# Output projection's weights: scaled and split beside the projection of v, kept in DRAM, loaded by the context steps

## The chip, the cores and the metric

The kernel runs on one core of a Trainium2 chip. Its time is the device time of one execution in microseconds (us), taken as the median of several runs. A profile is one more execution, recorded by the hardware profiler; its times are us from the first recorded instruction. The engines are PE (TensorE; PEld is its weight load), DVE (VectorE), ACT (ScalarE), POOL (GpSimd) and SP (SyncE), which issues nearly all transfers of this kernel, one after the other in a fixed order.

## The reference, cut to what matters

One layer of a trunk over 1024 latent tokens and 256 context tokens, width 1024. A normed and modulated input goes through one projection (`w_in`); its columns feed a short gated convolution (512 columns of output) and a bidirectional RWKV-7 scan (512 columns). Both outputs together go through the output projection `w_out`, and a gated residual follows; then a convolutional MLP. The gate `g1` comes from the modulation (`ada_w`).

```python
sh1, sc1, g1, sh2, sc2, g2 = split(silu(c) @ ada_w + ada_b)
hc = modulate(rms_norm(ctx, norm1_g), csh1, csc1)
_, ctx_states = mixer_block(hc, lp, (zero, zero), False)      # context: states only
hx = modulate(rms_norm(x, norm1_g), sh1, sc1)
out_x = concat([y_conv, y_rwkv]) @ w_out
x = x + g1 * out_x
x = x + g2 * conv_ffn(modulate(rms_norm(x, norm2_g), sh2, sc2))
return rms_norm(x, final_g)
```

Since g1 multiplies the columns of the product, the kernel multiplies it into the columns of `w_out` before the product.

## The kernel before, in words

Products that need full precision are made of three matmuls of rounded operands: a weight is split into a rounded high part (ACT cast) and the remainder (POOL subtraction), and so is the other operand.

Stages, in the order of the program:

1. Norms and the modulation's first half. The normed input lies in `hx` tiles.
2. The projections. `proj` runs one block of 128 columns over all tokens; `load_w` loads and splits its weights one block ahead (one buffer `wraw`, two of the split parts). A string `OR1` gives the order of the pieces: `k0` to `k3` (projection of k), `a` (an eighth of the modulation's second half), `u` and `x` (a third of the unit-norm of k; `x` takes the last third and then closes the pool `kn` that holds k), and `0` to `3` (projection of v). The gate g1 is written to DRAM by the first two `a` pieces.
3. `decays` and `invert`, for five groups of two token tiles each, the context's group first: elementwise chains per group of columns and direction, small matmuls, and the inversion of 32x32 triangles by 60 short DVE instructions in a row (lines 671 and 673). Their tiles lie in the pool `dq`. The rest of the projections (r, the gate, the convolution's three parts) is traced behind the first group and between, and its matmuls fill TensorE.
4. The steps of the scan (`steps`), each with one chunk per direction: products with the state (`ry`, line 761), copies, a second product (`pu`), its copy (`vu`), and the state's update (`S`, line 788). Four context steps come first, then sixteen latent steps. The output projection of the convolution's half (`conv_out`, product line 907, tile `pco`) and later that of the scan's half (`outp`, tile `po`) are cut into pieces that fill the latent steps.
5. The MLP and the final norm.

The weights of the output projection are made in stage 4. `w_raw(k)` loads block k of `w_out` (128 rows, 0.5 MB) into one of two buffers `xo`; `w_make(k)` multiplies by the gate (`gb1`, DVE line 900), casts (ACT line 901) and subtracts (POOL line 902). Blocks 0 and 1 are loaded ahead of the steps; after context step r, blocks 2r and 2r+1 are made, behind the step's last instructions on each engine (`behind`), and the next two are loaded. Blocks 0 to 3 serve the convolution's half and lie in the pool `cp_` on the right, blocks 4 to 7 the scan's half in the pool `ow` on the left.

Memory is two stacks of pools, one from each end of SBUF. On the right, above the tiles of stage 1 and 2 that stay, stand `hcp` (context's input), `ad` (modulation) and above these `kn`, 60,288 bytes per partition by the sizes of its tiles, until `x` closes it. On the left, `dq` takes about 100,000 bytes and reaches into the places of `hcp`, `ad` and `kn`. A tile that is put over older ones waits for their last readers (`reuse_waits="tile"`). The order of the instructions on each engine is set when the program is built: a planner with costs of its own takes the ready instruction that was traced first.

Of the kernel before, what the change touches and what calls it, by code (L numbers as in the profile page):

```python
# [8 lines left out]
F32 = mybir.dt.float32  # L9
F32R = mybir.dt.float32r  # L10
AF = mybir.ActivationFunctionType
ALU = mybir.AluOpType
# [3 lines left out]
D = 1024  # L16
# [20 lines left out]
XB, XT = 2, 3  # L37
# [6 lines left out]
B2 = ((2, 3), (1, 6))  # L44
B3 = (7, 5)
PA, PL1 = (0,), (6,)
OR1 = "k0 k1 a k2 a k3 a u 0 a u a 1 u a a x 2 a 3"
B4 = dict(pm=(5, 7), px=(0, 4), ph=(4, 0))
CL, AR = 2, 3
PJ1 = (1, 2, 3)  # L50
# [37 lines left out]
def hybrid_kernel(  # L88
# [7 lines left out]
    V, A, G, PE, SY = nc.vector, nc.scalar, nc.gpsimd, nc.tensor, nc.sync  # L96
# [12 lines left out]
    dr = ctx_.enter_context(tc.tile_pool(name="dr", bufs=1, space=DRAM))  # L109
# [44 lines left out]
    vd = dr.tile([NT, 128, 512], F32, name="v_dram")  # L154
    sgd = dr.tile([128, T], F32, name="sg_dram")
    yd = dr.tile([8, 128, 512], F32, name="y_dram")
    ycd = dr.tile([4, 128, T], F32, name="yc_dram")
    gd = [dr.tile([1, D], F32, name=f"g_dram{i}") for i in range(2)]
    x2d = dr.tile([8, 128, D], F32, name="x2_dram")
# [46 lines left out]
    with ExitStack() as s2:  # L206
# [106 lines left out]
        while n_ < NT:  # L313
# [4 lines left out]
                               in1=prm[:, P_N1:P_N1 + 8].unsqueeze(2).to_broadcast([128, 8, 2]), op0=ALU.add, op1=ALU.mult)  # L318
        for g, (t0, n, w) in enumerate(segs3):
            for q in range(2):  # L320
                o = [seg_tile(g, q, i, F32R) for i in range(2)]
# [45 lines left out]
    sa = ExitStack()  # L367
# [15 lines left out]
    for d in range(2):  # L383
# [3 lines left out]
        for i, src in enumerate((rw_w_up, rw_a_up)):  # L387
            raw = stg()
# [3 lines left out]
            r = slice(64 * i, 64 * i + 64)  # L392
# [64 lines left out]
    def ada_rest():  # L457
# [33 lines left out]
            yield  # L491
        V.scalar_tensor_tensor(out=gs2, in0=modc[:, 3, :, 0], scalar=1.0, in1=prm[:, P_N2:P_N2 + 8], op0=ALU.add, op1=ALU.mult)

    pa_ = Banks(pa=PA)
    ada_ = ada_rest()
    un = unit_k()
    for o in OR1.split():
        if o == "u":
            next(un)
        elif o == "a":  # L500
            next(ada_, None)
        elif o == "x":
            next(un, None)
            kn_.close()
        elif o[0] == "k":
            k_cols(int(o[1:]))
        else:
            v_cols(int(o))
# [197 lines left out]
    @contextmanager  # L706
    def behind():

        with ExitStack() as q:
            for i in chain.values():  # L710
                q.enter_context(tc.issue_after(i.ins))
            yield
# [162 lines left out]
    sa = ExitStack()  # L875
    cp_ = sa.enter_context(tc.tile_pool(name="co", bufs=1, side="right", reuse_waits="tile"))
# [7 lines left out]
    ow = so.enter_context(tc.tile_pool(name="ow", bufs=1, side="left", reuse_waits="tile"))  # L884


    gb1 = cp_.tile([128, D], F32, name="gb1")
    SY.dma_start(gb1, gd[0].to_broadcast([128, D]))

    wts, raws_ = {}, {}  # L890

    def w_raw(k):
        raws_[k] = cp_.tile([128, D], F32, name="xo", bufs=XB)
        SY.dma_start(raws_[k], w_out[0, 128 * k:128 * k + 128, :])

    def w_make(k):

        raw = raws_[k]
        hl = wts[k] = [(cp_ if k < 4 else ow).tile([128, D], F32R, name=f"w{'hl'[i]}{k}") for i in range(2)]
        V.tensor_tensor(out=raw, in0=raw, in1=gb1, op=ALU.mult)  # L900
        A.copy(hl[0], raw)
        G.tensor_tensor(out=hl[1], in0=raw, in1=hl[0].bitcast(F32), op=ALU.subtract)

    def product(po, hl, w, sl):
        for k in range(4):
# [132 lines left out]

    stages = {"m": mix, "o": outp, "h": to_h2}
    ppc = Banks(ry=B2[0], pu=B2[1])  # L1040
    w_raw(0)
    w_raw(1)
    for r in range(4):
        steps(ring, [(0, r // 2, r % 2), (1, 1 - r // 2, 1 - r % 2)], ppc, 1)

        with behind():
            w_make(2 * r)
            w_make(2 * r + 1)
        if r < 3:
            w_raw(2 * r + 2)  # L1050
            w_raw(2 * r + 3)
        if r == 1:
            pend.append(conv_out())
            next(pend[0])
# [197 lines left out]
```

## Time and profile before

| | us |
|---|---|
| median of 3 runs | 1689.11 (1687.71 to 1690.62) |
| profiled execution | 1681.7 |
| its span, first to last instruction | 1679.9 |
| PE busy | 1534.4 (91%) |
| DVE busy | 1154.1 (69%) |
| ACT busy | 619.9 (37%) |
| POOL busy | 567.3 (34%) |

The profiled execution is 7.4 us under the median of the runs. The shares are means over stages with different limits: the DVE's 69% holds stretches where it is never idle and the MLP, where TensorE is. What a change in one stage is worth has to be read from that stage.

### The profile page before, as it was taken

How to read it: one execution, taken by the hardware profiler on the slowest of the kernel's cores; microseconds unless marked ns; L12 is line 12 of the kernel's file. 1: busy time of each engine (PE TensorE's matmuls, PEld its weight loads, DVE VectorE, ACT ScalarE, POOL GpSimd, SP SyncE). 2: the span in 40 equal slices, each digit the busy share in tenths (PEclk: the TensorE clock that was granted, in tenths of full speed). 3: DMA queues.
4: the chain of work that ended last, by engine and by line, in shares of the span. 5: the costliest groups of instructions: out<-in, count | busy, mean ns of one | idle time of the engine just before them, and what ended most of it. 6: DMA issues, size and time to landing. Idle time of an engine off the chain costs nothing.

```text
span 1679.9 us, 27373 instructions
## 1 busy us (share of the span) xinstructions
PE 1534.4 (91%) x10567; PEld 1240.1 (74%) x10567; DVE 1154.1 (69%) x1783; ACT 619.9 (37%) x1158; POOL 567.3 (34%) x498
## 2 busy tenths in 40 slices
PE   7699999989898876898788899999999999999997
PEld 2588678767776766787666678888888887788886
DVE  5964526899899987445677678777777777346645
ACT  2654325535545235443454322221112112325323
POOL 2454413433233222412545232222222222545643
PEclk9699999989998867999899999999999999999999
DMA  9396556556665685989643112111111111533531
GB/s 322 110 290 203 173 169 189 170 164 212 209 198 167 219 261 177 335 262 278 187 133 116 51 50 62 41 49 51 50 51 51 51 40 48 190 101 124 175 93 59
DMA packets 233171, 246.93 MB, mean 147 GB/s; under 512 B 18496, under 2 KB 171685, under 8 KB 233041
## 3 DMA queue, kind: packets, MB, share of 16 engines
q1 hardware_dynamic: 232624, 245.02, 46.9%
q8 instruction: 84, 1.38, 0.4%
q14 instruction: 47, 0.38, 0.1%
q0 software_dynamic: 416, 0.16, 0.0%
HBM read 178.79 MB, written 66.33 MB: 146 GB/s over the span
## 4 chain that ended last, share of the span: by engine, by line
PE 51%; DVE 13%; ACT 2%; DMA 2%; issue 2%; POOL 1%; SPq 0%; DVEq 0%; ACTq 0%; POOLq 0%
PE pf L1105 26%; PE pf L1185 13%; PE po L907 2%; PE pco L907 2%; DVE acc L1152 2%; PE pj L355 2%; DVE ti L673 2%; PE ry L761 2%; DVE tmp L671 1%; PE ps L785 1%; PE pu L773 1%; DMA car<-ar_dram 1%; PE ry L753 1%; DVE S L788 1%; PE ry L794 1%
## 5 line engine op out<-in xcount | busy, mean ns | idle before, releaser
L1105 PE MATMUL pf<-h,fhi 128*128 128x512 f32 x1408 | 385.6, 391 | 7.6 <-DVE act L1157 4.1
L1105 PEld LDWEIGHTS pf<-h,fhi 128*128 128x128 f32 x1408 | 265.2, 189 | 64.3 <-DVE act L1157 4.5
L355 PE MATMUL pj<-hx,whi 128*128 128x512 f32 (+1 forms) x976 | 299.7, 385 | 3.0 <-DVE hx L329 1.9
L1152 DVE SCALAR_TENSOR_TENSOR acc<-gp,prm,acc 128x1024 f32<-128x1024 f32 x176 | 272.9, 1552 | 6.0
L106 POOL TENSOR_TENSOR flo<-fraw,fhi 128x1024 fp32r<-128x1024 f32 x50 | 123.2, 2465 | 305.9 <-ACT fhi L105 305.9
L1105 PE MATMUL pf<-h,flo 128*128 128x512 f32 x704 | 224.3, 391 | 0.0
L355 PEld LDWEIGHTS pj<-hx,whi 128*128 128x128 f32 x976 | 180.8, 192 | 39.6 <-issue 3.9
L355 PE MATMUL pj<-hx,wlo 128*128 128x512 f32 (+1 forms) x488 | 187.0, 383 | 0.0
L1185 PE MATMUL pf<-dhi,ahl 128*128 128x512 f32 x640 | 163.1, 389 | 0.3 <-DVE ahl L1177 0.3
L1177 DVE TENSOR_TENSOR ahl<-act,ahl 128x512 fp32r<-128x512 f32 x44 | 86.2, 1970 | 100.1 <-ACT ahl L1176 100.1
L1105 PEld LDWEIGHTS pf<-h,flo 128*128 128x128 f32 x704 | 132.7, 189 | 27.8 <-POOL flo L106 0.2
L105 ACT CAST fhi<-fraw 128x1024 fp32r<-128x1024 f32 x50 | 52.7, 1054 | 267.7 <-issue 162.5
L1185 PEld LDWEIGHTS pf<-dhi,ahl 128*128 128x128 f32 x640 | 120.0, 188 | 25.6 <-DVE ahl L1177 0.8
L106 POOL TENSOR_TENSOR dlo<-fraw,dhi 128x1024 fp32r<-128x1024 f32 x40 | 98.5, 2466 | 92.2 <-ACT dhi L105 91.4
L106 POOL TENSOR_TENSOR wlo<-wraw,whi 128x1024 fp32r<-128x1024 f32 x26 | 64.4, 2477 | 132.9 <-ACT whi L105 131.9
L1150 DVE TENSOR_SCALAR acc<-gp,prm 128x1024 f32<-128x1024 f32 x22 | 42.5, 1932 | 97.2 <-ACT gp L1142 97.2
L355 PEld LDWEIGHTS pj<-hx,wlo 128*128 128x128 f32 x488 | 93.6, 192 | 16.9 <-issue 0.8
L1185 PE MATMUL pf<-dlo,ahl 128*128 128x512 f32 x320 | 89.1, 389 | 0.0
L651 POOL TENSOR_TENSOR car<-car,pcs 128x512 f32<-128x512 f32 (+1 forms) x38 | 39.6, 1055 | 140.8 <-DMA car<-ar_dram 114.7
L105 ACT CAST dhi<-fraw 128x1024 fp32r<-128x1024 f32 x40 | 41.9, 1050 | 105.0 <-PE pf L1185 87.5
L602 PE MATMUL px<-arO,kbO 64*128 64x128 f32 (+1 forms) x640 | 65.5, 308 | 13.2 <-DVE xrO L606 8.9
L602 PEld LDWEIGHTS px<-arO,kbO 64*128 64x128 f32 x640 | 52.5, 205 | 31.4 <-issue 23.2
(292 smaller groups left out, 2620.1 us busy)
## 6 DMA issues: line engine op xcount, KB each, us to landing
araw<-in_ada_w_dram SPq DMA_DIRECT2D x48, 512.0 KB, 5.7
fraw<-in_ffn_w_up_dram SPq DMA_DIRECT2D x46, 512.0 KB, 3.9
fraw<-in_ffn_w_down_dram SPq DMA_DIRECT2D x44, 512.0 KB, 3.6
wraw<-in_w_in_dram SPq DMA_DIRECT2D x26, 512.0 KB, 4.6
lu<-lu_dram SPq DMA_DIRECT2D x20, 512.0 KB, 4.2
kb_dram<-kbT SPq DMA_DIRECT2D x40, 256.0 KB, 4.3
xa_dram<-xa SPq DMA_DIRECT2D x20, 512.0 KB, 4.4
cxa<-xa_dram SPq DMA_DIRECT2D x40, 256.0 KB, 4.2
```

The source lines that it names most:

```text
L105: A.copy(hi, src)
L106: G.tensor_tensor(out=lo, in0=src, in1=hi.bitcast(F32), op=ALU.subtract)
L355: PE.matmul(p[:, :n], w[:, k, :], hsl(i, k, t0, n), start=(k == 0 and first), stop=(k == 7 and last))
L602: PE.matmul(px[:, ch, i, 0:w], kbO[r, i, 2 * ch:2 * ch + 2, :].rearrange("p s n -> p (s n)"), rhs, start=True, stop=True)
L651: F3.tensor_tensor(out=self.ar, in0=self.ar, in1=self.pc.to_broadcast(list(self.ar.shape)), op=ALU.mult)
L673: V.tensor_tensor(out=ti[:, j + 1:32, 0:j], in0=ti[:, j + 1:32, 0:j], in1=tv, op=ALU.add)
L907: m = PE.matmul(po, hl[:, a_, k, :], w[k][b_][:, sl], start=(k == 0 and f), stop=(k == 3 and l))
L1105: PE.matmul(pts[hf], w[:, k, :], h2[hf][i_][:, k, :], start=(k == 0 and f), stop=(k == 7 and l))
L1150: V.tensor_scalar(out=acc, in0=src, scalar1=wcol, scalar2=prm[:, P_FB + f:P_FB + f + 1], op0=ALU.mult, op1=ALU.add)
L1152: V.scalar_tensor_tensor(out=acc, in0=src, scalar=wcol, in1=acc, op0=ALU.mult, op1=ALU.add)
L1177: V.tensor_tensor(out=hl[:, 1, :], in0=asl, in1=hl[:, 0, :].bitcast(F32), op=ALU.subtract)
L1185: PE.matmul(pd[i], hl[:, a_, 128 * q:128 * q + 128], w[w_][:, 512 * nh:512 * nh + 512], start=(f == 0 and s_), stop=(f == NF - 1 and l_))
```

## The change

A new function, `out_weights`, stands in the order of the projections behind the last third of the unit-norm (`x`) and the third block of v, ahead of the last `a` and the last block of v. It opens a pool `wm` in the stack place that `kn` has left: the gate's row spread over 128 partitions (`gb1`, 4 KB per partition), two buffers for a raw block (4 KB each) and two for a split block (8 KB each), 28,672 bytes in all. For each of the eight blocks it loads the raw rows, multiplies on DVE, casts on ACT, subtracts on POOL and stores both parts to a new DRAM tensor `wo_dram` (1 MB per block). The pool is closed with `ad`, ahead of `decays`. The context steps only load the split blocks, one transfer of 1 MB each, straight into their final tiles; the DVE, ACT and POOL work after each step, the two raw buffers and the `behind` orders are gone.

```diff
-OR1 = "k0 k1 a k2 a k3 a u 0 a u a 1 u a a x 2 a 3"
+OR1 = "k0 k1 a k2 a k3 a u 0 a u a 1 u a a x 2 w a 3"
...
+    wod = dr.tile([8, 128, 2, D], F32, name="wo_dram")
...
+    def out_weights():
+
+        wm = sa.enter_context(tc.tile_pool(name="wm", bufs=1, side="right", reuse_waits="tile"))
+        gb1 = wm.tile([128, D], F32, name="gb1")
+        SY.dma_start(gb1, gd[0].to_broadcast([128, D]))
+        for k in range(8):
+            raw = wm.tile([128, D], F32, name="wor", bufs=2)
+            SY.dma_start(raw, w_out[0, 128 * k:128 * k + 128, :])
+            hl = wm.tile([128, 2, D], F32R, name="wol", bufs=2)
+            V.tensor_tensor(out=raw, in0=raw, in1=gb1, op=ALU.mult)
+            A.copy(hl[:, 0], raw)
+            G.tensor_tensor(out=hl[:, 1], in0=raw, in1=hl[:, 0].bitcast(F32), op=ALU.subtract)
+            SY.dma_start(wod[k], hl.bitcast(F32))
...
-    gb1 = cp_.tile([128, D], F32, name="gb1")
-    SY.dma_start(gb1, gd[0].to_broadcast([128, D]))
-
-    wts, raws_ = {}, {}
-
-    def w_raw(k):
-        raws_[k] = cp_.tile([128, D], F32, name="xo", bufs=XB)
-        SY.dma_start(raws_[k], w_out[0, 128 * k:128 * k + 128, :])
-
-    def w_make(k):
-
-        raw = raws_[k]
-        hl = wts[k] = [(cp_ if k < 4 else ow).tile([128, D], F32R, name=f"w{'hl'[i]}{k}") for i in range(2)]
-        V.tensor_tensor(out=raw, in0=raw, in1=gb1, op=ALU.mult)
-        A.copy(hl[0], raw)
-        G.tensor_tensor(out=hl[1], in0=raw, in1=hl[0].bitcast(F32), op=ALU.subtract)
+    wts = {}
+
+    def w_load(k):
+        hl = (cp_ if k < 4 else ow).tile([128, 2, D], F32R, name=f"w{k}")
+        SY.dma_start(hl.bitcast(F32), wod[k])
+        wts[k] = [hl[:, i] for i in range(2)]
...
-    w_raw(0)
-    w_raw(1)
+    w_load(0)
+    w_load(1)
     for r in range(4):
         steps(ring, [(0, r // 2, r % 2), (1, 1 - r // 2, 1 - r % 2)], ppc, 1)
-
-        with behind():
-            w_make(2 * r)
-            w_make(2 * r + 1)
         if r < 3:
-            w_raw(2 * r + 2)
-            w_raw(2 * r + 3)
+            w_load(2 * r + 2)
+            w_load(2 * r + 3)
```

## Rows read from the trace of the kernel before

**Rows 1.** Stretches: length, busy per engine (instructions), granted clock, DMA share, GB/s

```profile
236.00:248.00 12.00, 12.00 (x56) 10.01 (x55) 0.23 (x1) 3.33 (x4) 2.39 (x1) 1.00 0.85 288
248.00:305.00 57.00, 57.00 (x355) 46.03 (x354) 35.51 (x72) 33.48 (x67) 18.31 (x34) 1.00 0.60 176
305.00:590.00 285.00, 253.11 (x2175) 203.98 (x2175) 270.98 (x625) 130.52 (x246) 94.69 (x146) 0.92 0.64 193
590.00:602.00 12.00, 10.67 (x178) 9.32 (x174) 6.00 (x13) 4.34 (x6) 1.24 (x2) 0.51 0.98 277
602.00:652.00 50.00, 28.06 (x476) 25.09 (x478) 47.68 (x84) 17.97 (x35) 14.71 (x10) 0.63 0.65 205
667.00:695.00 28.00, 21.86 (x318) 17.87 (x316) 12.60 (x19) 12.41 (x24) 11.83 (x7) 0.94 1.02 348
```

**Rows 2.** Groups of DVE instructions in 602 to 652: busy, mean ns, idle before

```profile
L900 DVE TENSOR_TENSOR xo<-xo,gb 128x1024 f32<-128x1024 f32 x4 | 4.7, 1222 | 0.1
```

**Rows 3.** Timeline of DVE, inversion: start, length, line, tile, shape

```profile
607.68 0.32 DVE L673 TENSOR_TENSOR ti<-ti,tmp 128x150 f32<-128x150 f32 x1
...
619.62 2.44 DVE L671 TENSOR_TENSOR tmp<-ti 128x240 f32<-128x240 f32 x1
...
622.81 1.72 DVE L673 TENSOR_TENSOR ti<-ti,tmp 128x240 f32<-128x240 f32 x1
...
626.49 0.41 DVE L673 TENSOR_TENSOR ti<-ti,tmp 128x238 f32<-128x238 f32 x1
...
639.10 2.36 DVE L673 TENSOR_TENSOR ti<-ti,tmp 128x150 f32<-128x150 f32 x1
...
642.54 2.31 DVE L673 TENSOR_TENSOR ti<-ti,tmp 128x130 f32<-128x130 f32 x1
```

**Rows 4.** Timeline of POOL: the first two subtractions; two more start at 638.85 and 642.32

```profile
619.28 4.98 POOL L902 TENSOR_TENSOR wl<-xo,wh 128x1024 fp32r<-128x1024 f32 x2 [10.14 <-ACT wh L901]
```

**Rows 5.** Timeline, latent steps: PE's state product; DVE's multiplication with the wait ahead

```profile
677.55 2.02 PE L761 MATMUL ry<-S,car 128*128 128x128 f32 x16 [2.07 <-DVE S L788]
...
688.97 2.55 DVE L900 TENSOR_TENSOR xo<-xo,gb 128x1024 f32<-128x1024 f32 x1 [1.31 <-DMA xo<-in_w_out_dram]
...
694.94 2.05 PE L761 MATMUL ry<-S,car 128*128 128x128 f32 x16
706.39 2.05 PE L761 MATMUL ry<-S,car 128*128 128x128 f32 x16
```

**Rows 6.** Timeline of POOL and of SP's queue where `dq` follows `kn`

```profile
235.63 0.15 POOL L570 MEMSET P<- 128x4 f32 x2 [6.78 <-PE pb L440]
...
236.26 0.33 SPq L442 DMA_DIRECT2D kk_dram<-kkr  x1
236.65 0.59 SPq L531 DMA_DIRECT2D dxl<-xl_dram  x1
```

**Rows 7.** SP's queue where the tiles of `conv_out` follow `dq`

```profile
666.47 1.01 SPq L701 DMA_DIRECT2D xa_dram<-xa  x2
...
668.21 3.58 SPq L918 DMA_DIRECT2D x<-in_x_dram  x3
```

**Rows 8.** Timeline: multiplications of blocks 0 and 1, the load into the freed buffer

```profile
616.90 2.36 DVE L900 TENSOR_TENSOR xo<-xo,gb 128x1024 f32<-128x1024 f32 x2
...
621.81 2.82 SPq L894 DMA_DIRECT2D xo<-in_w_out_dram  x2
```

**Rows 9.** Tile xo: issue to landing of its transfers, all of them

```profile
DMA to landing us min/median/max: 3.8/6.2/8.4
```

**Rows 10.** Groups of DVE instructions of the convolution's columns, whole span

```profile
L841 DVE TENSOR_TENSOR cu<-pj,cu 128x512 f32<-128x512 f32 x8 | 5.5, 686 | 1.3 <-PE pj L355 1.2
L843 DVE TENSOR_SCALAR cy<-cu,prm 128x1024 f32<-128x1024 f32 x4 | 3.9, 972 | 0.0
L845 DVE SCALAR_TENSOR_TENSOR cy<-cu,prm,cy 128x1024 f32<-128x1024 f32 x8 | 10.2, 1275 | 0.0
L849 DVE TENSOR_TENSOR cy<-pj,cy 128x512 f32<-128x512 f32 x8 | 5.4, 681 | 0.1
```

More of the change, by code (lines that the diff above doesn't have):

```diff
@@ L504, in hybrid_kernel @@
             kn_.close()
+        elif o == "w":
+            out_weights()
         elif o[0] == "k":
```

## The prediction, made before the changed kernel was run

> **What bounds the kernel now.** I read the page for the two stages that the change touches, then cut the span into stretches with one limit each, and only then looked at single instructions. The page's means say little here: the DVE's 69% is made of stretches at 98% and stretches at 45%. In the stretches [rows 1] the reader should compare PE's and DVE's busy time with the length. From 236 to 305 TensorE is full (12.00 of 12, 57.00 of 57) and DVE has room (0.23 of 12, then 35.5 of 57): projections are the limit and the context's decays run at their pace. From 305 to 590 DVE works 271 of 285 us, TensorE 253. So DVE is the limit there, and it stays it until 652 (47.7 of 50), while the last inversion and the context steps share it. Between them lie 12 us with DVE half idle and DMA at 0.98. From 667 to 695 DMA stands at 1.02 (348 GB/s), and no engine is full.
>
> **What is removed.** Of the eight blocks, four are made inside the DVE's full stretch. Their multiplications take 4 x 1.22 = 4.9 us, with 0.1 us of idle time ahead of them [rows 2]: that is path. POOL's four subtractions cost DVE more than that. During them an instruction of the inversion that takes 0.32 to 0.41 us takes 2.44, 1.72, 2.36 and 2.31 [rows 3, 4]. The four are 2.0 + 1.3 + 2.0 + 2.0 = 7.4 us longer than their like. Together -12.3 us; the bounds are -4.9 (if the stretching has another cause) and -12.3. The ACT casts lie beside and count nothing. Blocks 6 and 7 are made in the latent steps: DVE's multiplication waits for its transfer, and the copies of the step are queued behind it. The step from 677.55 to 694.94 takes 17.4 us, the next one 11.4 [rows 5]; without the multiplications I let the first fall to the second, -5.9 us, with bounds 0 and -5.9, since DMA is full there [rows 1] and may hold the step anyway.
>
> **What is moved, and where it lands.** The pass issues 8 multiplications (9.8 us), 8 casts, 8 subtractions and 17 transfers on SP's queue. As work it would cost nothing: DVE is free in 236 to 248 and TensorE is the limit [rows 1]. (Without that cover it would cost the 9.8 us and the stretching of whatever DVE does beside the subtractions.) What counts is the memory it stands in. `wm` takes the stack place of `kn`, and `dq`, with all tiles of the decays, comes over the same place later. The trace shows both halves of this. POOL's first memset of a decay tile (P) waits 6.8 us for a matmul of the unit-norm, which reads a tile of `kn` (bc8); by the sizes of the tiles, bc8 ends 17,280 bytes from the end of `kn` that stays, so P lies inside the 28,672 bytes of `wm` too. And the first load of the decays is issued 0.39 us behind the last store of `kn` [rows 6], though what it loads was written long before; the loads of `conv_out` follow the last store of `dq` in the same way [rows 7]. I read this as: the planner gives out a pool's place only when the last instruction of the pool beneath has been issued. Then `wm` begins at about 237, and the decays begin when the last store to `wo_dram` has been issued.
>
> How long is the pass? A raw buffer turns over in a load and 4.9 us (multiplication at 616.90, next load into the buffer at 621.81 [rows 8]). The load took 3.8 to 8.4 us, median 6.2 [rows 9]. Four rounds on each of two buffers: 4 x (6.2 + 4.9) = 44.4 us; 35 and 53 at the ends. I take the median, since the pass fills DMA as its old place did. So the decays start at 282 in place of 237: **+45 us** (36 to 54). As traffic the pass is 25 pieces of 0.524 MB, 13.1 MB, which at the 348 GB/s of [rows 1] is 38 us, inside those ends. The Trainium skill, page "SBUF — State Buffer", section "Summary: rules for kernel authors", says to reckon transfers between HBM and SBUF at about 358 GB/s; by that alone the pass would be 37 us (an estimate) and the forecast 8 us lower. The trace's best stretch, 348 GB/s, agrees with that figure, but the pass is a chain of loads and instructions, so I keep the chain.
>
> Part of this comes back. TensorE does not stop in the pause: 56 matmuls in 12.00 us [rows 1] make a column of 48 some 10.3 us, so 45 us put the projections 4.4 columns ahead. DVE's work on the convolution's 12 columns is 5.5 + 3.9 + 10.2 + 5.4 = 25.0 us [rows 10], 2.1 per column; 4.4 of them leave the full stretch: -9 us (0 to -9). DVE's idle time from 305 to 652 is 14.0 + 6.0 + 2.3 = 22 us [rows 1]; with 45 us less of TensorE's work beside it some of this closes: -5 us (0 to -22; I stay near zero, as most waits there are for copies and transfers that remain). The rest of the pause stays, because DVE is full from 305 on and has no other room to catch up.
>
> **What is added later.** SP loses nine transfers and gets eight, each twice as large. `cp_` opens when the last projection is done, and nothing holds blocks 1 to 3 back any more, where the two raw buffers did: 4.19 MB in place of 1.57 in a stretch with DMA at 0.98. The 2.6 MB more are 9.5 us at its 277 GB/s [rows 1]; I count +2 (0 to 9.5), as the chain needs only some of what is queued behind. Blocks 4 to 7 lie in `ow`, over `dq`, so by the reading of [rows 7] they come all together at the end of the inversion, just where DMA is full: 3.1 MB more, 9 us at 348 GB/s. In SP's queue the chunks of the next steps and the rows of x stand behind them, and DVE's residual add, with the state's update behind it, waits for x. I count +3 (0 to 9).
>
> **The sum.** 45 - 9 - 5 - 12.3 - 5.9 + 5 = +17.8 us on the profiled execution, 1681.7, gives 1699.5. That execution is 7.4 us under the median of the runs; put back on, 1707.
>
> **The rivals.**
> 1. *The pass hides, and the kernel is faster.* For it: the work is covered (DVE idle, TensorE full), and tiles of `kn` come free one by one, so that the planner could start the pass earlier and let the decays take places that the pass has left or never used. It decides at one point: whether the decays' first load is issued ahead of the last store to `wo_dram`, by so much that DVE has its usual work from 248 on. Then -12.3 - 5.9 + 5 and some 2 us for DVE's stretched instructions: -11, so 1678. Against it: [rows 6, 7]. The Trainium skill's page "SBUF — State Buffer", section "Who interferes with whom", speaks for this rival: "DMA never contends with a compute engine", so 16 MB more traffic would slow no instruction. The trace does not contradict it: where DMA is at 0.98, engines wait for data, they do not run slower. Chance 0.18.
> 2. *The pause is absorbed.* If DVE's full stretch has more give than I think (all 22 us of idle time close), the sum is 45 - 9 - 22 - 12.3 - 5.9 + 5 = +1, so 1690. For it: TensorE is at 89% in that stretch and will be relieved. Against it: DVE's own 95% there. Chance 0.12.
> 3. *It costs more.* The full 54 us of the slowest loads, with stores in SP's queue that wait for POOL while weight loads stand behind them, and nothing of the idle time back: 54 - 9 - 12.3 - 5.9 + 10 = +37, so 1726. Chance 0.10.
>
> **How the numbers follow.** My forecast, a pause carried mostly to the end, has 0.60, at 1707, by itself from about 1695 to 1721 (no idle time back: +32). A measurement of this kernel can tell some 0.2% (3.4 us) from no change. Slower by more: 0.60 + 0.10 = 0.70; within it 0.12; faster 0.18. For 8 in 10 the range goes from 1684, which leaves most of the first rival out, to 1724, which leaves out half of the third.
>
> **What would show it.** Right: on SP's queue the first load of `xl_dram` directly behind the last store to `wo_dram`, near 280; DVE nearly idle until about 290 but for eight multiplications; DVE full from some 350 on. In the steps no instruction of the inversion above 1.5 us, and the inversion's end 10 to 25 us later than 652. The second latent step shorter than 17.4 us. Wrong: decays that start before 260 (rival 1), an inversion that ends within a few us of its old time though the decays started late (rival 2), or a first latent step that waits for x longer than before, which would put the price into DMA.

## The result, and the profile after

| | before | after |
|---|---|---|
| median of the runs, us | 1689.86 (1687.71 to 1693.30) | 1729.94 (1728.35 to 1733.60) |
| profiled execution, us | 1681.7 | 1730.15 |
| its span, us | 1679.9 | 1728.2 |

The ratio is 1.025, with a 95% interval of 1.023 to 1.027 (the two medians by themselves give 1.024): the changed kernel is 40 us slower. The prediction had the side (slower, 0.70) and missed the size: 1707, with a range that ended at 1724. The profiled execution of before lies 8.2 us under the median of these four runs, and under every other run of this kernel on record (1683.1 to 1695.2); that of after lies at its median. So differences between the two traces are some 8 us larger than those of the medians (48 against 40).

First the stretches of after, as in [rows 1]: start and end, length, busy time of PE, PEld, DVE, ACT, POOL (instructions), granted clock, DMA share, GB/s.

```profile
251.00:295.00 44.00, 44.00 (x196) 36.46 (x195) 8.18 (x6) 15.77 (x19) 27.06 (x14) 1.00 0.97 345
295.00:350.00 55.00, 55.00 (x313) 45.09 (x313) 33.89 (x63) 26.16 (x53) 18.39 (x27) 1.00 0.59 179
350.00:500.00 150.00, 135.34 (x1063) 108.27 (x1063) 140.27 (x315) 63.24 (x121) 53.55 (x77) 0.97 0.56 172
500.00:550.00 50.00, 36.61 (x452) 30.74 (x445) 46.57 (x119) 24.18 (x49) 13.74 (x27) 0.69 0.88 293
550.00:600.00 50.00, 29.79 (x412) 26.09 (x412) 34.49 (x81) 21.42 (x39) 13.63 (x26) 0.61 0.94 288
600.00:650.00 50.00, 39.83 (x268) 33.34 (x268) 49.09 (x136) 21.92 (x46) 14.86 (x24) 0.60 0.60 172
655.00:692.00 37.00, 24.33 (x483) 21.73 (x477) 33.99 (x78) 13.13 (x29) 4.54 (x4) 0.73 0.59 190
708.00:750.00 42.00, 31.72 (x402) 26.04 (x399) 10.77 (x21) 12.29 (x28) 3.83 (x4) 0.87 1.04 358
```

The first line is the pass: TensorE full, DMA full, DVE at 8 of 44. The second looks like the 57 us from 248 in [rows 1], 47 us later. The fifth line is the surprise: DVE, forecast to be full from 350 on, is idle for 15.5 of 50 us, with DMA at 0.94. The last line is the place of the first latent steps: 358 GB/s, no engine full.

SP's queue of after around the pass (start, length, line, transfer), which answers [rows 6]:

```profile
239.32 0.33 SPq L443 DMA_DIRECT2D kk_dram<-kkr  x1
239.70 0.44 SPq L499 DMA_DIRECT2D gb<-g_dram  x1
240.24 0.87 SPq L502 DMA_DIRECT2D wor<-in_w_out_dram  x2
...
251.82 0.33 SPq L507 DMA_DIRECT2D wo_dram<-wol  x1
...
291.89 0.32 SPq L507 DMA_DIRECT2D wo_dram<-wol  x1
294.24 0.38 SPq L339 DMA_DIRECT2D wraw<-in_w_in_dram  x1
294.68 0.73 SPq L548 DMA_DIRECT2D dxl<-xl_dram  x1
```

Before, 0.4 us lay between the last store of `kk_dram` and the decays' first load [rows 6]. Now it is 294.68 - 239.32 = 55.4 us, and in between stands the whole pass. The load is issued 58.0 us later than before; 3.1 of these lie ahead of the pass.

The line of the pass's multiplications, with the idle time of DVE ahead of them (us, times):

```profile
L504 DVE TENSOR_TENSOR wor<-wor,gb x8: 1212/1240/2564, 245.7 to 287.1; 128x1024 f32<-128x1024 f32 x8
its engine sat idle before it (us, times) until:
  DMA wor<-in_w_out_dram: 28.4, 6
  POOL wlo L106: 8.7, 1
```

The multiplications wait mostly for their own loads: 28.4 us of idle time ahead of them, in six waits.

The end of the last inversion (its last stream transposition, DVE), in before and in after:

```profile
649.26 1.94 DVE L679 STREAM_TRANSPOSE rti<-ti 128x1024 f32<-128x1024 f32 x1
```

```profile
690.53 1.92 DVE L696 STREAM_TRANSPOSE rti<-ti 128x1024 f32<-128x1024 f32 x1
```

So a delay of 58 us at the decays' start is 41 us here, and 48 us at the end of the span. TensorE's products with the state that begin the second to the fifth latent step of after; the second to the fourth of before are in [rows 5], and the fifth stands last here:

```profile
711.17 2.05 PE L778 MATMUL ry<-S,car 128*128 128x128 f32 x16
721.51 3.65 PE L778 MATMUL ry<-S,car 128*128 128x128 f32 x16
749.61 3.37 PE L778 MATMUL ry<-S,car 128*128 128x128 f32 x16
762.33 2.05 PE L778 MATMUL ry<-S,car 128*128 128x128 f32 x16
```

```profile
717.78 2.05 PE L761 MATMUL ry<-S,car 128*128 128x128 f32 x16
```

The second product is 33.6 us late, less than the inversion's end; the fifth is 44.6 us late. So some 3 of the 7 us are lost up to here and the other 4 behind it. The step that was forecast to become shorter did: 10.3 us in place of 17.4 [rows 5]. The next one takes 28.1 us in place of 11.4, and the three steps together 51.2 in place of 40.2.

DVE's residual add in that long step, with the wait ahead of it, and the longest such wait in before:

```profile
726.50 1.29 DVE L942 TENSOR_TENSOR x<-pco,x 128x512 f32<-128x512 f32 x2 [7.57 <-DMA x<-in_x_dram]
```

```profile
675.94 0.69 DVE L935 TENSOR_TENSOR x<-pco,x 128x512 f32<-128x512 f32 x1 [3.54 <-DMA x<-in_x_dram]
```

### The profile page after: what moved, and what is told of

It is laid out like the page before. It is cut to its first block, busy times and chain, and to the rows that moved or that the text cites. A ratio compares the mean times of both kernels' runs of the same rounds, so it can differ in the third digit from the quotient of the medians.

```text
span 1728.2 us, 27381 instructions
## 1 busy us (share of the span) xinstructions
PE 1559.1 (90%) x10567; PEld 1264.7 (73%) x10567; DVE 1139.8 (66%) x1783; ACT 618.3 (36%) x1155; POOL 572.5 (33%) x498
## 4 chain that ended last, share of the span: by engine, by line
PE 48%; DVE 10%; DMA 3%; ACT 1%; issue 1%; POOL 1%; DVEq 0%; SPq 0%; ACTq 0%; POOLq 0%
PE pf L1108 26%; PE pf L1188 12%; PE po L914 2%; PE pco L914 2%; PE ry L778 2%; DVE acc L1155 2%; DMA x<-in_x_dram 1%; PE ry L770 1%; DVE ti L690 1%; DVE tmp L688 1%; PE pu L790 1%; DVE S L805 1%; DMA cxr<-xr_dram 1%; PE ps L802 1%; PE ry L811 0%
## 5 line engine op out<-in xcount | busy, mean ns | idle before, releaser
L356 PE MATMUL pj<-hx,whi 128*128 128x512 f32 (+1 forms) x976 | 294.8, 382 | 5.4 <-DVE hx L330 3.0
L1108 PEld LDWEIGHTS pf<-h,flo 128*128 128x128 f32 x704 | 133.3, 189 | 28.1 <-POOL flo L106 0.5
L356 PEld LDWEIGHTS pj<-hx,wlo 128*128 128x128 f32 x488 | 92.9, 190 | 16.7 <-issue 0.6
L619 PE MATMUL px<-arO,kbO 64*128 64x128 f32 (+1 forms) x640 | 72.9, 343 | 16.7 <-DVE xrO L623 13.1
L619 PEld LDWEIGHTS px<-arO,kbO 64*128 64x128 f32 x640 | 59.8, 237 | 32.1 <-issue 23.3
```

The lines of the kernel that those rows point to most:

```text
L356: PE.matmul(p[:, :n], w[:, k, :], hsl(i, k, t0, n), start=(k == 0 and first), stop=(k == 7 and last))
L619: PE.matmul(px[:, ch, i, 0:w], kbO[r, i, 2 * ch:2 * ch + 2, :].rearrange("p s n -> p (s n)"), rhs, start=True, stop=True)
L1108: PE.matmul(pts[hf], w[:, k, :], h2[hf][i_][:, k, :], start=(k == 0 and f), stop=(k == 7 and l))
```

## The experiments

Two theories stood against each other. A: the pass is the price, since the decays wait for the memory in which it stands. B: the loads of 1 MB blocks are the price, since they fill DMA ahead of what the steps need. In the runs "pass alone", "no pass" and "early pass" the letters mean these two; every other expectation defines an A and a B of its own. Each kernel ran beside the kernel before on the same chip; ratios go against that.

| kernel | median, us | ratio to before | 95% interval |
|---|---|---|---|
| changed kernel | 1729.94 | 1.0251 | 1.0229 to 1.0273 |
| pass alone | 1728.99 | 1.0258 | 1.0238 to 1.0277 |
| no pass | 1690.63 | 1.0022 | 1.0008 to 1.0035 |
| early pass | 1702.68 | 1.0105 | 1.0069 to 1.0142 |
| blocks 4 to 7 traced later | 1732.61 | 1.0279 | 1.0255 to 1.0302 |
| no pass, blocks 0 to 3 held | 1686.67 | 0.9990 | 0.9973 to 1.0007 |
| no pass, all blocks held | 1682.50 | 0.9969 | 0.9951 to 0.9987 |
| early pass, all blocks held | 1684.10 | 0.9973 | 0.9955 to 0.9991 |
| changed, ring held | 1729.44 | 1.0228 | 1.0192 to 1.0265 |
| changed, ring and blocks held | 1715.21 | 1.0164 | 1.0119 to 1.0209 |
| pass on ACT's queue | 1719.30 | 1.0199 | 1.0179 to 1.0220 |
| half the store | 1719.64 | 1.0204 | 1.0185 to 1.0222 |

**The pass alone.** The kernel before, with the pass in it and its result unused:

```diff
-OR1 = "k0 k1 a k2 a k3 a u 0 a u a 1 u a a x 2 a 3"
+OR1 = "k0 k1 a k2 a k3 a u 0 a u a 1 u a a x 2 w a 3"
+        elif o == "w":
+            out_weights()
```

> The kernel before with the pass added as the change has it, and its result used by nobody: the context steps still load, multiply and split the blocks themselves. So it has the change's cost without its gain. Theory A (the decays wait for the memory of the pass, and that delay is carried to the end): in the trace of the changed kernel the first load of xl_dram is issued at 294.7 in place of 236.7, and nothing of it came back by the end of the inversion but what was removed from the context steps. Then 1689 + 45 to 55 = 1735 to 1745, slower than the changed kernel (1730) by some us. Theory B (the delay is mostly absorbed by the stretches behind it, and the loads of 1 MB blocks are the price): not above 1705. First load of xl_dram near 292 to 295 in both.

The ratio, 1.0258, is that of the changed kernel: the pass alone costs as much as the whole change. Theory B's limit, 1705, is far off. Theory A holds for the pass, though the median, 1729, is under its 1735 and not above the changed kernel's: some of the delay does come back, and the removed work is worth nothing net, as the next run shows. The first load of `xl_dram` on SP's queue and the end of the last inversion on DVE, in this trace:

```profile
290.34 0.73 SPq L548 DMA_DIRECT2D dxl<-xl_dram  x1
```

```profile
700.00 1.91 DVE L696 STREAM_TRANSPOSE rti<-ti 128x1024 f32<-128x1024 f32 x1
```

53.7 us late at the decays' start, 50.7 at the inversion's end, 47.0 at the end of the span. All that DVE's full stretch gave back is 3 us.

**No pass.** The changed kernel without it, the blocks loaded from another tensor of the same size:

```diff
-OR1 = "k0 k1 a k2 a k3 a u 0 a u a 1 u a a x 2 w a 3"
+OR1 = "k0 k1 a k2 a k3 a u 0 a u a 1 u a a x 2 a 3"
-        SY.dma_start(hl.bitcast(F32), wod[k])
+        SY.dma_start(hl.bitcast(F32), xld[:, :, 0:D])
```

> The changed kernel without the pass: the context steps load 1 MB per block from xl_dram in place of wo_dram, so the output projection's weights hold other numbers and the multiplication, the split and the store are left out altogether. Same loads, same tiles, same order of the steps. Theory A (the pause is the price, the removed work a gain): the inversion's end comes 10 to 14 us earlier than in the kernel before (651), the step in which blocks 4 to 7 are loaded stays some 28 us long, and the time is 1675 to 1690. Theory B (the loads are the price): 1705 or more, with DVE idle for 10 us and more in the last 50 us ahead of the last inversion.

Neither: 1691, between the two. The inversion's end does not come earlier (649.33), and the longest of the first latent steps takes 21.1 us. The work of eight multiplications, casts and subtractions is gone, nothing was put in its place but loads, and the kernel is no faster. DVE's timeline of this kernel shows why:

```profile
612.23 0.75 DVE L623 TENSOR_TENSOR xrO<-px,cst 128x256 f32<-128x256 f32 x2 [4.67 <-DMA xr_dram<-xrO]
612.90 1.90 DVE L682 STREAM_TRANSPOSE ti<-xb 128x1024 f32<-128x1024 f32 x1
...
649.33 1.94 DVE L696 STREAM_TRANSPOSE rti<-ti 128x1024 f32<-128x1024 f32 x1
```

The same transposition at the start of the last inversion, in before:

```profile
602.04 1.97 DVE L665 STREAM_TRANSPOSE ti<-xb 128x1024 f32<-128x1024 f32 x1 [0.41 <-ACT xb L661]
```

The last inversion begins 10.9 us later than before. From the end of the fourth inversion to there DVE waits 6.8 us for stores of the last group's decays to land, so that their buffers are free (3.7 us in before), and 7.4 us for products of TensorE (1.8 in before); DMA stands at 1.05 in 602 to 613. Then inversion and context steps take 36.4 us in place of 47.2. The gain of some 11 us is there, and it is taken away just ahead of it; whether the loads do that is what the next run asks. The stretching by POOL's subtractions is gone too: 30 instructions of a line of the inversion, minimum, median and maximum in ns, first in before (590 to 700), then here.

```profile
L671 DVE TENSOR_TENSOR tmp<-ti x30: 168/372/2440, 604.1 to 647.0; 128x30 f32<-128x30 f32 x2, 128x58 f32<-128x58 f32 x2, 128x84 f32<-128x84 f32 x2, 128x108 f32<-128x108 f32 x2
```

```profile
L688 DVE TENSOR_TENSOR tmp<-ti x30: 167/358/730, 614.9 to 647.1; 128x30 f32<-128x30 f32 x2, 128x58 f32<-128x58 f32 x2, 128x84 f32<-128x84 f32 x2, 128x108 f32<-128x108 f32 x2
```

The Trainium skill, page "SBUF — State Buffer", section "Who interferes with whom", says that a DVE instruction with two inputs in SBUF contends with a GpSimd instruction that reads SBUF. The maximum, 2440 ns with subtractions beside it and 730 without, agrees.

**Blocks 0 to 3 held.** The kernel without the pass, with these loads behind a copy that waits for a context step:

```diff
-    def w_load(k):
+    def w_load(k, behind_):
         hl = (cp_ if k < 4 else ow).tile([128, 2, D], F32R, name=f"w{k}")
+        if behind_ is not None:
+            G.tensor_copy(hl[:, 0, 0:8], behind_)
...
+        if r < 2:
+            w_load(2 * r, Sd[0][:, 0, 0:8])
+            w_load(2 * r + 1, Sd[0][:, 0, 0:8])
```

> The kernel without the pass (blocks loaded from xl_dram, multiplication, split and store left out, as before), and one thing more: the loads of blocks 0 to 3 are held behind the first two context steps (a copy of 8 columns of the state into the block's tile, ahead of its load), so that they no longer stand in DMA while the last group's decays run. Theory A (in the kernel without the pass these 4 MB make DVE wait for a store of xr_dram from 606.0 to 612.2, and the last inversion begins at 613.0 in place of 602.0, which takes back all that the removed work gives): the inversion begins at 600 to 605 and ends (last rti copy) at 637 to 642 in place of 649, and the time is 7 to 12 us under that of the kernel without the pass (1691), some 1679 to 1684, below the kernel before. Theory B (the last stretch has another limit, and the removed work lay beside it): the inversion's end stays at 647 to 652 and the time at 1687 to 1694.

Theory A holds for the place: the inversion begins and ends where it was expected to, and the loads account for 7.8 of the 10.9 us.

```profile
605.13 1.94 DVE L682 STREAM_TRANSPOSE ti<-xb 128x1024 f32<-128x1024 f32 x1
...
640.81 1.95 DVE L696 STREAM_TRANSPOSE rti<-ti 128x1024 f32<-128x1024 f32 x1
```

The end comes 8.5 us earlier than without the hold. Only 4 of these reach the end of the kernel (1686.7, not the 1679 to 1684 expected): the step between the state products at 667.16 and 692.93 takes 25.8 us, with blocks 4 to 7 and the rows of x in the same stretch.

**All blocks held.** Blocks 4 to 7, too, each behind a residual add:

```diff
+            if 1 <= n <= 4:
+                w_load(3 + n, xts_[t][:, 0:8])
```

> As the kernel before this one, and blocks 4 to 7 are held as well: each behind the residual add of one of the second to fifth tiles of the convolution's half, so some 30 to 80 us later, and one at a time. Still without the pass and with other numbers for the weights. Theory A (the 4 MB stand ahead of the x rows): the latent step of 19.3 us falls to 11 to 15 and the time is 4 to 8 us under that of the kernel with blocks 0 to 3 held alone. Theory B (the x rows and the chunks fill DMA there by themselves): no more than 2 us.

The end of the last inversion:

```profile
639.18 1.97 DVE L696 STREAM_TRANSPOSE rti<-ti 128x1024 f32<-128x1024 f32 x1
```

The state products now stand at 663.93, 679.33 and 691.44: 25.8 us became 15.4, and the median fell by 4.2 us, the lower end of theory A. Later steps take most of the lead back: against the kernel with blocks 0 to 3 held the products are 13.6 us ahead at 679.33 and 3.7 us at 758.66, with a step of 17.4 us between. So without any pass, and with the loads out of the way, the removed work is worth 0.3%, 5 us. That is all that the change could win with these holds.

**Blocks 4 to 7 traced later.** In the changed kernel the loads were moved behind the latent steps 4 to 7 in the program:

```diff
-        if r < 3:
+        if r < 1:
             w_load(2 * r + 2)
             w_load(2 * r + 3)
...
+        if 4 <= r < 8:
+            w_load(r + 0)
```

> The changed kernel with one thing moved: blocks 4 to 7 are loaded one by one behind the latent steps 4 to 7, no longer together at the end of the inversion; they are first used behind step 10. Theory A (these 4 MB stand in SP's queue and in DMA ahead of the x rows for which DVE's residual add, and the state's update behind it, waits): the step of 28.1 us (721.5 to 749.6) falls to 14 to 18, and the time is 1715 to 1722. Theory B (DMA is full there anyway with the chunks of the steps and the x rows): the step stays above 24 us and the time within 4 us of 1730.

Inconclusive as it was meant: the planner takes what is ready, and the loads were issued at 726.94 to 733, only 14 us later, still in the full stretch. The long step did shrink (715.43, 734.53, 753.40, 766.53), but three steps together take 51.1 us, as in the changed kernel (711.17 to 762.33: 51.2). I read this as: in a full stretch it is the bytes that count, not which of them comes first. Hence the copies that wait, above. One thing this run does show, the wait for x:

```profile
725.86 1.29 DVE L942 TENSOR_TENSOR x<-pco,x 128x512 f32<-128x512 f32 x2 [7.64 <-DMA x<-in_x_dram]
```

It ends before the first of the four blocks is issued and is as long as in the changed kernel. So the wait does not need these blocks ahead of it.

**Early pass.** The same pass in 12 KB on the left, in 16 pieces of 512 columns, in the projections of k and v:

```diff
+    we = sa.enter_context(tc.tile_pool(name="we", bufs=1, side="left", reuse_waits="tile"))
-OR1 = "k0 k1 a k2 a k3 a u 0 a u a 1 u a a x 2 w a 3"
+OR1 = "k0 a k1 a k2 w k3 w a w u w 0 w a u w a w 1 w u a a x 2 a 3"
```

> The changed kernel with the same pass elsewhere: 12 KB per partition on the left, free during the projections of k and v, in 16 pieces of 512 columns, from behind k2 on, so that nearly all of it is through when the unit-norm ends. Nothing else differs. Theory A (place in memory and time of the pass): the first load of xl_dram is issued 0 to 15 us later than in the kernel before, and the time is 1680 to 1700, as for the kernel without the pass plus that delay. Theory B (16 MB more traffic and the pieces on SP's queue are what costs, wherever they stand): the projections of k and v take 10 us and more longer, and the time stays above 1710.

The median, 1703, is a little above theory A's range and far under theory B's. Most of the price is gone with the place; the same 13 MB of traffic elsewhere cost far less. (The trace is of the slowest of the four runs, 1712.) The waits of DVE from 80 to 256 (us, times, longest) have this line:

```profile
DVE wor L505 <- DMA wor<-in_w_out_dram: 29.4, 9, 4.8
```

The pass's multiplications wait for their loads with the unit-norm queued behind them on DVE. The last store of `kk_dram` comes at 248.31 in place of 236.26, and the first load of `xl_dram` at 255.66, 19 us late, a little more than expected; here too it follows the last store of the pass (252.87). That the waits are what delays the unit-norm is not shown: in the last run below they fall to 11.9 us, and the last store of `kk_dram` comes no earlier (250.11).

**Pass on ACT's queue.** Is it the memory that the decays wait for, or the place in SP's queue?

```diff
-            SY.dma_start(wod[k], hl.bitcast(F32))
+            A.dma_start(wod[k], hl.bitcast(F32))
```

(and so for the two loads in the function)

> The changed kernel with the pass's 17 transfers issued from ACT's queue in place of SP's. Theory A (the decays wait for the memory that the pass stands in, when its last instruction has been issued): the first load of xl_dram is still issued behind the last store to wo_dram, at 288 to 298, and the time is 1722 to 1740. Theory B (they wait in SP's queue, in which the pass's stores stand ahead of their loads and wait for POOL): the load comes at 236 to 250, and the time falls to 1685 to 1700.

ACT's queue, then SP's, of this kernel:

```profile
290.07 0.33 ACTq L507 DMA_DIRECT2D wo_dram<-wol  x1
```

```profile
292.42 0.38 SPq L339 DMA_DIRECT2D wraw<-in_w_in_dram  x1
292.85 1.03 SPq L548 DMA_DIRECT2D dxl<-xl_dram  x1
```

SP has nothing of the pass in its queue, and its load still follows the last store, 55.3 us behind the last store of `kk_dram` (237.60). So it is not the order in SP's queue, and the place in memory, as [rows 6, 7] were read, is what is left. The Trainium skill, page "DMA: Bandwidth & Descriptors", section "Issuing engines are not separate DMA queues", says that transfers run on the same 16 engines whoever issues them; 55.3 us here and 55.4 from SP's queue agree. The median, 1719, is 10 us under the changed kernel's and in neither range; the gain appears between the decays' third and fourth group, and I did not find its cause.

**Half the store.** What makes the pass 55 us long?

```diff
-            SY.dma_start(wod[k], hl.bitcast(F32))
+            SY.dma_start(wod[k, :, 0], hl[:, 0].bitcast(F32))
-        SY.dma_start(hl.bitcast(F32), wod[k])
+        for i in range(2):
+            SY.dma_start(hl[:, i].bitcast(F32), wod[k, :, 0])
```

> The changed kernel with half the store: the pass stores the rounded half of a block only, 0.5 MB in place of 1 MB, and the context steps load that half into both places, in two transfers of 0.5 MB; the remainder is made, but left out of the product. It asks what sets the length of the pass (239.7 to 294.7). Theory A (DMA: 345 GB/s in 251 to 295, of which the projections' weights and the stores of r are a part, so 4.2 MB less are 12 us): the first load of xl_dram at 280 to 285, the time 8 to 12 us under the changed kernel's 1730. Theory B (the chain of a buffer: load, multiplication, cast, subtraction, next load): the load comes at 290 to 295, the time within 4 us of 1730.

SP's queue at the end of the pass:

```profile
281.53 0.55 SPq L507 DMA_DIRECT2D wo_dram<-wol  x1
283.44 0.32 SPq L845 DMA_DIRECT2D sg_dram<-stg  x1
283.81 0.58 SPq L548 DMA_DIRECT2D dxl<-xl_dram  x1
```

283.81 less 236.61, the last store of `kk_dram`, is 47.2 us, 8.2 less than with the full store, and the median falls by 10. DMA's share in 252 to 280 falls from 1.02 to 0.75. Not all of the 8.2 us is traffic: the store of the rounded half no longer waits for POOL's subtraction, which takes some 3.5 us off the end (the last subtraction ends at 285.03, the last store is issued at 281.53). So the traffic of the full store is worth some 5 us of the pass. With the full store 18.3 MB move between 238 and 295; 13.1 MB of them are the pass's, the other 5.2 MB the projections' own weights and stores.

**Ring held.** Why did DVE's full stretch give so little back? In the changed kernel the third inversion's last transposition stands at 559.4 against 519.8, 40 us late in place of 58, and the fourth's at 649.1 against 588.4, 61 us late: 18 us had come back, and then were lost again.

```diff
+    def hold():
+        z = wp.tile([128, 8], F32, name="zh")
+        for g in (1, 2):
+            for q in range(2):
+                for i in range(2):
+                    G.tensor_tensor(out=z, in0=hxt[g, q, i][:, 0, 0:8].bitcast(F32), in1=groups[6][:, 0, 0, 0, 0:8], op=ALU.add)
...
+            if ti == 6 and n == 0:
+                hold()
```

> The changed kernel with one thing more: eight small POOL additions read the projections' input tiles and wait for the first direction of the last group's decays, so that the memory of ring and co comes free only then, and the chunks of the steps and the blocks 0 to 3 are loaded after 595 in place of 514 to 557. It asks why the delay of 55 us, of which 17 us had come back by the third inversion (559.4 against 519.8), was lost again: between the loads of xl_dram at 498.2 and 584.3 a group takes 86 us, where it took 69 in the kernel before. Theory A (the early loads fill DMA, and the decays wait for their own): the second of these loads comes at 567 to 576, DVE is idle for less than 8 us in 550 to 600, and the time falls to 1715 to 1723. Theory B (the projections are used up at 515, TensorE has no filling and its granted clock stands at 0.5 to 0.76, so the small matmuls take twice as long): the load comes at 580 to 587 and the time stays at 1726 to 1736.

The stretches of this kernel, columns as above:

```profile
550.00:600.00 50.00, 32.59 (x396) 28.03 (x394) 48.15 (x126) 25.76 (x50) 13.87 (x33) 0.57 0.62 192
600.00:650.00 50.00, 38.48 (x531) 32.18 (x530) 36.92 (x89) 20.37 (x35) 11.79 (x22) 0.64 1.04 334
```

Theory B falls: with a granted clock of 0.57, lower than the 0.61 of the changed kernel, DVE works 48.15 of 50 us in 550 to 600 in place of 34.49. What had stopped it were the early loads: the projections end at 515 in place of 569, their memory goes to `ring` and `co`, and 4 MB of blocks and the chunks of the steps are loaded while two groups of decays are still to come. In the changed kernel DVE's longest wait in 550 to 600 (6.1 us, for ACT) goes back over TensorE to a load (us, times, longest):

```profile
PE plo L573 <- DMA dxl<-xl_dram: 8.6, 1, 8.6
```

Another 7.5 us there are waits for other products of TensorE (`px`), which the trace does not follow to a load. With the ring held the load of the last group's `xl_dram` is issued at 551.2 in place of 584.3, earlier than expected. But the time stays in theory B's range and does not fall as theory A said: the held loads come in 600 to 650, DMA stands at 1.04 there, DVE idles 13 us, and the last inversion ends where it did (689.76). The loss has only changed its place.

The kernel with the pass alone has the same pattern and loads no split block: 37 us late at the third inversion's end, 56 at the fourth's, DVE idle for 11 us in 550 to 600, with DMA at 0.71. The hold was not run in that kernel, so there the cause is not shown.

**Ring and blocks held.** So the blocks were held as well, by the diffs above together:

> The changed kernel with all three holds and the pass where the change has it: ring and co come free behind the first direction of the last group's decays, blocks 0 to 3 are loaded behind the first two context steps, blocks 4 to 7 behind residual adds of the convolution's half. Nothing is left out. Hold of the ring alone: the fourth inversion ended at 619.8 in place of 649.1, but DVE then stood idle for 13 us in 600 to 650 with DMA at 1.04, and the last inversion ended at 689.8 as before. Theory A (the pause would be given back in part, were it not for the 4 MB of blocks in that stretch): DVE busy above 46 of 50 us in 600 to 650, the last rti copy at 668 to 680, the time 1706 to 1718. Theory B (DVE's work up to there is what it is, and the whole pause is carried on): the last rti copy at 684 to 690 and the time at 1722 to 1730.

A stretch of this kernel, and DVE's last transposition:

```profile
600.00:650.00 50.00, 40.08 (x556) 33.97 (x558) 44.35 (x111) 23.33 (x44) 10.33 (x22) 0.67 0.98 304
```

```profile
673.16 1.94 DVE L696 STREAM_TRANSPOSE rti<-ti 128x1024 f32<-128x1024 f32 x1
```

DVE's 44.35 is a little under the 46 expected; the inversion's end and the time, 1715 (its four runs lie between 1706 and 1718), are in theory A's range. Against the kernel without the pass and with the blocks held, the pass now costs 1.0164 / 0.9969 = 1.020, 33 us of its 55. The two traces say the same: the decays' first load is 56 us later (291.79 against 235.80), the inversion's end 34. So the stretch can give back 22 us of a late start when these loads are held, though DMA stands at 0.98 in 600 to 650 even so.

**Early pass, all blocks held.** The pass begins earlier and loads further ahead, and the blocks are held as above:

```diff
-                raw = we.tile([128, 512], F32, name="wor", bufs=2)
+                raw = we.tile([128, 512], F32, name="wor", bufs=3)
-OR1 = "k0 a k1 a k2 w k3 w a w u w 0 w a u w a w 1 w u a a x 2 a 3"
+OR1 = "k0 a a k1 w k2 w k3 w a w u w 0 w a u w a w 1 u a a x 2 a 3"
```

> The whole change with its costs taken away one by one, nothing left out: the pass early, in 12 KB on the left (three raw buffers, the gate in two halves), and the loads of blocks 0 to 3 and of blocks 4 to 7 held as in the two kernels ahead of this one. Theory A (place of the pass, loads ahead of the last inversion, loads ahead of the x rows are the three prices): 1702.7 for the early pass alone, less 7 to 12 and 4 to 8: 1683 to 1692, about as fast as the kernel before. Theory B (they are not additive, the early pass costs its 12 us in the unit-norm and the rest stays): 1697 or more.

SP's queue around the end of the pass, and DVE's last transposition:

```profile
243.09 0.52 SPq L508 DMA_DIRECT2D wo_dram<-wol  x1
...
250.11 0.32 SPq L443 DMA_DIRECT2D kk_dram<-kkr  x1
250.48 0.58 SPq L553 DMA_DIRECT2D dxl<-xl_dram  x1
```

```profile
640.73 2.02 DVE L701 STREAM_TRANSPOSE rti<-ti 128x1024 f32<-128x1024 f32 x1
```

The pass is through before the unit-norm, and the decays' load follows the last store of `kk_dram` by 0.4 us again. It is 14.7 us later than in the kernel without the pass and with the blocks held (235.80), and at the inversion's end 1.6 us are left of that (639.18). The time, 1684, is in theory A's range: 0.27% (0.09 to 0.45) under the kernel before, and 2.7% under the changed kernel.

## Why the prediction was wrong, point by point

**The reading of the memory was right.** The decays' first load follows the last store of the pass, as [rows 6, 7] were read; the run with ACT's queue and the early pass leave no other cause that I know, though no run moves the pass in memory alone, at its time. Rival 1, by whose condition the load comes first, falls.

**The length of the pass was too short: 45, measured 55.** The chain of a buffer had the right shape and links that were too short: on SP's queue of after the four turns of the second buffer (its loads at about 240.7, then 254.58, 267.96 and 279.94, the last store at 291.89) take 51.2 us in place of 44.4, and 4.2 us at the two ends were not in the sum. The step that failed is the comparison with DMA: "13.1 MB, which at the 348 GB/s is 38 us, inside those ends". TensorE goes on in the pause, so its weights and results move too, 5.2 MB that the sum leaves out: 18.3 MB at 345 GB/s are 53 us. That such traffic runs there stood in [rows 1]: 176 GB/s in 248 to 305, the decays' loads included. Of the 10 us missed, half the store shows some 5 to be traffic; the other 5 are not shown apart. The upper end of the range, 54, was nearly the measured value, but for another reason, the slowest load of 8.4 us; the pass's loads took 6.1 us (median), as reckoned.

**What was to come back, -14 us, came to 3 by the inversion's end** in the pass alone, 7 by the end of the span. The columns did run ahead, as the prediction said: the convolution's last store comes at 515 in place of 569. What it did not see is what follows from that. The same columns hold the memory of `ring` and `co`; when they end early, the loads of the steps start early too, beside decays that are late. DVE's idle time of 15.5 us in 550 to 600 is the price in the changed kernel, and the runs with the ring and the blocks held show it (22 us come back there). The prediction said that `cp_` opens when the last projection is done, and did not put that beside its own forecast that the projections run ahead while the decays start 45 us late.

**The removed work, -12.3, was sized right.** By the kernel without the pass the last inversion and the context steps are 10.8 us shorter (36.4 in place of 47.2), and none of the inversion's short instructions there is above 1.5 us (1.1 at most). But **the loads of blocks 0 to 3, +2 with an end of 9.5, were mis-sized**: the last inversion begins 10.9 us later in that kernel, and holding them gives 7.8 of these back. I took a value near zero, as the chain would need only some of what is queued behind; the decays need a store to land before a buffer is free, and that waits with the rest (6.8 us of such waits in place of 3.7). In the kernel before two raw buffers kept these loads out of that place; what reads as a limit of the old kernel was a protection.

**The latent steps, -5.9 + 3, became +11** in the changed kernel (three steps of 51.2 us in place of 40.2, over which the lateness grows from 33.6 to 44.6) and +4.5 without the pass (675.91 to 720.61). The step with the raw blocks did lose its 5.9 us and more; the next one grew by 16.7. The prediction named what would show it wrong, a residual add that waits for x longer than before: it waits 7.6 us in place of 3.5. But its reason, blocks 4 to 7 ahead of x, is not shown: with these blocks issued behind it the wait is 7.64, and a load of x takes 8.7 us (median) from issue to landing, 8.5 in before. What is shown is that DMA is full there (358 GB/s), and that without the pass holding these blocks shortens a step by 10 us. Why x comes late in the changed kernel stays open.

**The sum.** The pass alone costs 47 us of span and the kernel without the pass 4; together 51, and the changed kernel has 48. In the forecast the same two parts were 45 - 9 - 5 = 31 and -12.3 - 5.9 + 5 = -13: the one missed by 16 us, the other by 17. One bracket of the prediction is misread: "no idle time back: +32" leaves out the columns' 9 us as well; without the idle time alone the sum is +23, 1712. Rival 2, with the pause absorbed, falls with the pass alone. Rival 3, 1726 with 0.10, came nearest: the pause at its upper end, nothing of the idle time back, the loads dear. The stores in SP's queue ahead of weight loads, which it also named, are not what made the pass long: from ACT's queue it is 55.3 us. It deserved more: all its ends hang on one thing, DMA, so they were not independent mishaps that seldom meet. The range should have gone through that case whole and not to half of it.

## What to carry to other kernels

A stage that takes a place in memory between two pools can cost most of its own length (47 of 55 us here), however idle its engines are: ask what is allocated over it, and who waits for that. Count the bytes of every stretch into which transfers are moved together with those that are there already, and ask what a stage that now ends earlier lets start: loads that run ahead stand in the way of work that has fallen behind. Before a throttle is removed (two raw buffers), look what it keeps apart.

## What was not expected of the hardware

Where DMA was full it mostly moved about the same: 345 GB/s in the pass (1 MB stores among them), 334 in 600 to 650 with the ring held, 358 in the latent steps of after. But a high share alone does not say so: at 0.98 it moved 277 GB/s in 590 to 602 of before [rows 1], and 304 in 600 to 650 with the ring and the blocks held. And a granted clock of 0.57 in 550 to 600 (the mean of stretches at 1.2 and 2.4 GHz) did not keep DVE from working 48 of 50 us there: I take it that the small matmuls of the decays had room at that clock; no run was made for that alone.
